# Turning V with VectorE's block transposes instead of TensorE's, in a two-layer trunk

## The chip, the cores and the metric

One Trainium2 core runs the whole program. The metric is the device time of one execution in microseconds, lower is better. The data engines are TensorE (PE; its weight loads are shown apart as PEld), VectorE (DVE), ScalarE (ACT) and GpSimd (POOL). SyncE (SP) issues most loads, GpSimd's queue issues the stores.

## The reference

Input x is 1024 tokens by 1024 features in fp32. Two residual layers follow each other, each with an RMS norm in front:

```python
# layer 0: short gated convolution, width 2048
b, c, u, z = split(h @ w_in, 4)
y = b * conv3(c * u) * silu(z);  x = x + y @ w_out
# layer 1: dilated sliding-window attention, 3 groups (dilation 1, 4, 16) x 16 heads x 64
qkv, z = h @ w_in
q = rms_norm(q) ; k = rms_norm(k)                     # per head
out_g, lse_g = softmax(q k^T / 8 + bias_g) v          # within each group's window and residue classes
o = sum_g softmax_g(lse) * out_g                      # groups merged by their denominators
x = x + (o * silu(z)) @ w_out
```

## The kernel before

Activations lie feature-major: 128 features on the partitions, 1024 tokens along them, worked on in two halves of 512 tokens. The program has four stages: the projections of the convolution layer, its output projection, the projections of the attention layer, and the attention with the last projection.

**Projections.** They are fp32 products made of three reduced-precision ones (high times high, high times low, low times high), and the 2 x 2 blocks of weights and activations are multiplied in Strassen's way with seven products instead of eight. The list `pairs` of the attention layer holds 40 entries. An entry makes two 128-column outputs (`col` 0 and 1) for both halves of the tokens, with seven products of twelve matmuls each (L302, L304, L305). `("qk", hp, g)` gives the query and the key of head pair hp and dilation group g (a unit), `("v", k)` gives the values of two consecutive units, `("z", k)` two gates. The rhythm is qk, qk, v, twelve times, with z entries between. `strassen` runs the products of entry n and makes the weights of entry n + 1 meanwhile: GpSimd forms sums (`sr`, L277), ScalarE the high parts (L165), VectorE the low parts (L166). The products end in VectorE's additions (L314) and ScalarE's copies (L310). The products 4 and 3 of an entry run during the next one.

`between(n, at)` is called after each product and issues the work that is due: `norm` of a qk entry two entries later (per-head norm: a matmul with `swap` into PSUM tile "st", a chain of small VectorE operations, then four times a block transpose of the scales, L712, and the multiplication L724 into the output tile, which GpSimd's queue stores to `qkd`), and four `turn`s of a v entry, also two entries later.

**The values.** Each half of a v output is multiplied by the row scale R1 (1/rms of the token) as it comes out: L684, three of four on GpSimd, one on VectorE, into `spare()`, which is the first half of block tile "blkc"; the norm's output tiles (`out_tile`) are the second half of it. `turn(col, q)` then brings V to token-major: four TensorE transposes of 128 x 128 (L737) into one PSUM bank ("st" for q = 0, "pp" for q = 1), a copy to a tile "f" (ScalarE L742 or VectorE L740), and a store to `vd` (L743). `blk` picks the 128 tokens of a block; for dilation 4 these are every fourth word.

**The row scale.** `stats(1)` computes `rtok` for the second half of the tokens by a chain of VectorE operations on 4 columns (L63 to L67); `spread(1, rtok)` lets TensorE spread it over the partitions into the one bank "st" (L104), which ScalarE copies to R1 (L106). `spread(1, ms2)` does the like for the norm's constant, and `norm` uses the same bank.

**Attention.** `load_v` loads V of a unit, and TensorE loads slices of it as weights, 64 features of one block (L978 for dilations 1 and 4, L971 for 16).

TensorE's order is the order of the code. In the projections the order on the other engines is set by a scheduler that simulates the program, in the attention all orders are written out. The rows of the trace for the groups of 272 matmuls are those of `product`.

Of the kernel before, what the change touches and what calls it, by code (L numbers as in the profile page):

```python
# [19 lines left out]
P = 128  # L20
# [9 lines left out]
G = 3  # L30
# [5 lines left out]
def trunk(ctx: ExitStack, tc: tile.TileContext, a, out):  # L36
# [83 lines left out]
    vd = dram.tile([HP, G, 2, P, HALF], F32, name="vd")  # L120
# [7 lines left out]

    def blk(t, g, b):
        if g == 0:  # L130
            return t[:, b * P:(b + 1) * P]
        if g == 1:
            return t.rearrange("p (n s c) -> p c n s", n=2, c=4)[:, b // 2, b % 2]
        return t[:, b * P:(b + 1) * P]

    with tc.tile_pool(name="wq", bufs=1) as wq, tc.tile_pool(name="sle", bufs=1) as sle, \
# [371 lines left out]
        with tc.tile_pool(name="ev", bufs=1, side="right", reuse_waits="tile") as ev, tc.tile_pool(name="xb", bufs=1, side="right", reuse_waits="tile") as xb, \  # L508
# [150 lines left out]
            def pair(n, w):  # L659
# [4 lines left out]
                def got(col, hf, t, ps=None):  # L664
# [12 lines left out]
                    elif kind == "v":  # L677
                        vt = spare()[:, col * S + hf * HALF:col * S + hf * HALF + HALF]
                        eng, t, r = (nc.vector, ps, R1[:, cs]) if ps is not None else (nc.gpsimd, t, R1[:, cs])
                        if units[p[1] + col][1] == 2:  # L680
                            vt = spare()[:, col * S:col * S + S].rearrange("p (r x i) -> p i x r", r=4, x=4)
                            vt = vt[:, hf * 32:hf * 32 + 32]
                            t, r = (y.rearrange("p (i x r) -> p i x r", x=4, r=4) for y in (t, r))
                        eng.tensor_tensor(vt, t, r, op=OP.mult)  # L684
                    else:
                        if ps is not None:
                            t = ftile()
                            nc.vector.tensor_tensor(t, ps, R1[:, cs], op=OP.mult)
                        else:
                            nc.gpsimd.tensor_tensor(t, t, R1[:, cs], op=OP.mult)  # L690
                        nc.scalar.activation(t, t, AF.Silu)
                        nc.gpsimd.dma_start(zd[p[1] + col, :, cs], t)
# [36 lines left out]
                def turn(col, q):  # L729
                    hp, g = units[p[1] + col]  # L730
                    vt = spare()[:, col * S:col * S + S]
                    if q:
                        pv = cps.tile([P, 4, P], F32, name="pp", tag="pp")
                    else:
                        pv = cst.tile([P, 4, P], F32, name="st", tag="st")
                    for i in range(4):
                        nc.tensor.transpose(pv[:, i], blk(vt, g, 4 * q + i), ident)  # L737
                    o = ftile()
                    if q:
                        nc.vector.tensor_copy(o, pv.rearrange("p a b -> p (a b)"))  # L740
                    else:
                        nc.scalar.activation(o, pv.rearrange("p a b -> p (a b)"), AF.Copy)  # L742
                    nc.gpsimd.dma_start(vd[hp, g, q], o)  # L743
# [39 lines left out]
            def between(n, at):  # L783
# [3 lines left out]
                if n == 1 and at == 0:  # L787
                    stats(1, cst, sm)
                elif n == 2 and at == 2:
                    spread(1, rtok, cst)  # L790
                elif n == 1 and at == 6:
                    spread(1, ms2, cst)
# [30 lines left out]
    with tc.tile_pool(name="sp", bufs=1, space=PSUM) as sp, tc.tile_pool(name="ptp", bufs=2, space=PSUM) as ptp, \  # L823
# [23 lines left out]
        def load_v(hp, g):  # L847
            VS[hp, g] = ap.tile([P, 8, P], F32, name="V", tag="V", bufs=3)
            for q in range(2):
                nc.sync.dma_start(VS[hp, g][:, 4 * q:4 * q + 4].rearrange("p a b -> p (a b)"), vd[hp, g, q])  # L850
# [21 lines left out]
        def attention(hp, g):  # L872
# [24 lines left out]
            def make(js, first):  # L897
# [63 lines left out]
                def C():  # L961
# [4 lines left out]
                    for i, (x, j, vb, f, l) in enumerate(c):  # L966
                        for a in range(2) if g == 2 else ():
                            for s, hs in enumerate((lo, up)):
                                for h in range(2):
                                    rows = slice(64 * h, 64 * h + 64)  # L970
                                    nc.tensor.matmul(u["po", h][hs, (vb + a) * 64:(vb + a) * 64 + 64],  # L971
                                                     V[rows, vb + a, hs], pts[s][rows, i, 64 * a:64 * a + 64],
                                                     start=True, stop=True)
                        for s, hs in enumerate((lo, up)) if g < 2 else ():
# [3 lines left out]
                            nc.tensor.matmul(po[:, j % 4], V[:, vb, hs], pts[s][:, i], start=f, stop=l)  # L978
# [361 lines left out]
```

## Time and profile before

| | |
|---|---|
| median of three runs | 1951.64 us (1950.47 to 1955.07) |
| profiled execution, its span | 1951.91 us, 1950.1 us |
| TensorE, VectorE, ScalarE, GpSimd busy | 98%, 74%, 46%, 43% of the span |
| the turns, in the attention layer's projections | from 902 to 1610 us |
| attention and last projection | from some 1620 us to the end |
| 48 turns on TensorE (L737) | 192 transposes, 29.2 us busy |
| their copies | VectorE 24 x 686 ns, ScalarE 24 x 586 ns |
| stores of V | 48 of 256 KB, 554 ns each on GpSimd |

In a line of the timeline the first number is the start (us from the span's start), the second the duration, and the bracket the idle time before it with what ended it. Rows of the groups give count, busy us and mean ns, and then the idle time in front of them. In the rows by source line the three numbers are the shortest, median and longest duration in ns.

### The profile page before, as it was taken

Reading aid. Unit: us, or ns where it says so; the run is one execution under the profiler, and the core shown is the slowest. Engines: PE = TensorE matmul, PEld = TensorE weight load, DVE = VectorE, ACT = ScalarE, POOL = GpSimd, SP = SyncE. Lnnn points to the kernel's source line nnn. Section 1 sums busy time; section 2 is a strip of 40 time slices with the busy share of each in tenths; the row PEclk is TensorE's granted clock in tenths of the full one; section 3 lists DMA queues with packets and bytes.
Section 4 is the critical chain, followed back from the end, with each engine's and each line's share of the span. In section 5 each row is a group of like instructions: output and inputs, shape, how many; then the busy total and the mean of one; then the engine's idle time right before and its main releaser. Section 6 shows DMA issues by size and latency. Waiting matters only on the chain.

```text
span 1950.1 us, 30571 instructions
## 1 busy us (share of the span) xinstructions
PE 1906.7 (98%) x10894; PEld 1553.0 (80%) x10894; DVE 1443.7 (74%) x2770; ACT 892.3 (46%) x2031; POOL 847.5 (43%) x775
## 2 busy tenths in 40 slices
PE   8999999999999999989999999999999998889999
PEld 6888888888888888878888888888888886667777
DVE  7876766676666655777787588768877776899996
ACT  6433333333333444444444443444344437877780
POOL 0366666666665211424434443444343452333330
PEclk9999999999999999999999999999999999899999
DMA  6312232323223665422332322332232336887852
GB/s 196 121 58 89 88 96 83 99 74 103 76 87 102 222 208 187 140 89 101 106 111 103 114 98 102 115 108 99 92 124 87 130 126 225 251 278 228 245 158 87
DMA packets 117033, 253.79 MB, mean 130 GB/s; under 512 B 17726, under 2 KB 23070, under 8 KB 116880
## 3 DMA queue, kind: packets, MB, share of 16 engines
q1 hardware_dynamic: 93280, 176.89, 28.2%
q0 software_dynamic: 23600, 74.95, 11.3%
q8 instruction: 85, 1.39, 0.3%
q14 instruction: 68, 0.56, 0.1%
HBM read 192.53 MB, written 67.64 MB: 133 GB/s over the span
## 4 chain that ended last, share of the span: by engine, by line
PE 88%; DVE 4%; DMA 4%; ACT 2%; issue 2%; POOL 1%; SPq 0%; DVEq 0%; POOLq 0%; ACTq 0%
PE pp L302 22%; PE pp L304 22%; PE pp L305 22%; PE pp L554 3%; PE pp L555 3%; PE pp L553 3%; ACT xs L950 2%; DMA nld<-nl 2%; PE pp L375 1%; PE pp L376 1%; PE pp L377 1%; PE po L978 1%; PE pt L957 1%; DVE xs L944 1%; DMA ml<-nld 1%
## 5 line engine op out<-in xcount | busy, mean ns | idle before, releaser
L166 DVE TENSOR_TENSOR ws<-wr,ws 128x512 fp32r<-128x512 f32 x284 | 295.4, 1042 | 133.9 <-ACT ws L165 132.0
L165 ACT ACTIVATE ws<-wr 128x512 fp32r<-128x512 f32 x284 | 178.6, 630 | 388.6 <-PE pp L305 254.9
L165 ACT ACTIVATE ws<-sr 128x512 fp32r<-128x512 f32 x272 | 171.6, 631 | 365.9 <-PE pp L305 297.7
L277 POOL TENSOR_TENSOR sr<-wr 128x512 f32<-128x512 f32 x136 | 190.2, 1399 | 266.6 <-DMA wr<-in_wqk 76.5
L166 DVE TENSOR_TENSOR ws<-sr,ws 128x512 fp32r<-128x512 f32 x272 | 219.3, 810 | 84.2 <-ACT ws L165 81.8
L314 DVE TENSOR_TENSOR f<-pp,f 128x512 f32<-128x512 f32 x204 | 140.0, 686 | 105.7 <-PE pp L305 97.8
L950 ACT ACTIVATE xs<-xs,nl 128x256 f32<-128x256 f32 (+2 forms) x384 | 160.5, 424 | 0.0
L310 ACT ACTIVATE f<-pp 128x512 f32<-128x512 f32 x228 | 132.3, 580 | 9.3 <-PE pp L305 9.3
L277 POOL TENSOR_TENSOR sr<-wr,sr 128x512 f32<-128x512 f32 x68 | 88.8, 1306 | 67.9 <-issue 44.1
L944 DVE CUSTOM_DVE_ANT_0 xs<-ps,bt 128x256 f32<-128x256 f32 (+2 forms) x384 | 102.4, 326 | 11.1 <-ACT xs L950 4.4
L302 PE MATMUL pp<-blkf,ws 128*128 128x512 f32 x272 | 108.2, 398 | 0.7 <-ACT f L310 0.7
L302 PE MATMUL pp<-blka,ws 128*128 128x512 f32 x272 | 107.1, 394 | 0.7 <-ACT f L310 0.7
L302 PE MATMUL pp<-blkb,ws 128*128 128x512 f32 x272 | 107.4, 395 | 0.0
L302 PE MATMUL pp<-blkd,ws 128*128 128x512 f32 x272 | 107.3, 395 | 0.0
L305 PE MATMUL pp<-blkf,ws 128*128 128x512 f32 x272 | 106.2, 391 | 0.0
L304 PE MATMUL pp<-blkd,ws 128*128 128x512 f32 x272 | 106.2, 391 | 0.0
L305 PE MATMUL pp<-blkd,ws 128*128 128x512 f32 x272 | 106.1, 390 | 0.0
L304 PE MATMUL pp<-blkf,ws 128*128 128x512 f32 x272 | 106.1, 390 | 0.0
L305 PE MATMUL pp<-blke,ws 128*128 128x512 f32 x272 | 106.1, 390 | 0.0
L305 PE MATMUL pp<-blkb,ws 128*128 128x512 f32 x272 | 106.0, 390 | 0.0
L305 PE MATMUL pp<-blka,ws 128*128 128x512 f32 x272 | 106.0, 390 | 0.0
L302 PE MATMUL pp<-blke,ws 128*128 128x512 f32 x272 | 105.9, 389 | 0.0
(342 smaller groups left out, 5164.1 us busy)
## 6 DMA issues: line engine op xcount, KB each, us to landing
wr<-in_conv_w_in SPq DMA_DIRECT2D x128, 256.0 KB, 3.1
wr<-in_wqk SPq DMA_DIRECT2D x96, 256.0 KB, 3.3
qkd<-blkc POOLq DMA_DIRECT2D x48, 512.0 KB, 3.4
qk<-qkd SPq DMA_DIRECT2D x48, 512.0 KB, 5.4
wr<-in_conv_w_out SPq DMA_DIRECT2D x64, 256.0 KB, 3.2
f<-in_x SPq DMA_DIRECT2D x48, 256.0 KB, 4.4
wr<-in_wv SPq DMA_DIRECT2D x48, 256.0 KB, 3.3
vd<-f POOLq DMA_DIRECT2D x48, 256.0 KB, 2.3
```

The lines of the kernel that those rows point to most:

```text
L165: nc.scalar.activation(t[:, 0], src, AF.Copy)
L166: nc.vector.tensor_tensor(t[:, 1], src, t[:, 0].bitcast(F32), op=OP.subtract)
L277: nc.gpsimd.tensor_tensor(t, x, y, op=op)
L302: nc.tensor.matmul(ps, w[:, 0, ws], b[:, k, 0], start=new and k == 0, stop=False, skip_group_check=not new)
L304: nc.tensor.matmul(ps, w[:, 0, ws], b[:, k, 1], start=False, stop=False, skip_group_check=not new)
L305: nc.tensor.matmul(ps, w[:, 1, ws], b[:, k, 0], start=False, stop=end and k == 3, skip_group_check=not new)
L310: nc.scalar.activation(t, ps, AF.Copy)
L314: nc.vector.tensor_tensor(m, ps, m, op=OP.add)
L553: nc.tensor.matmul(ps[dt], w[:, 0, ws], b[:, k, 0], start=(q == k == 0), stop=False)
L554: nc.tensor.matmul(ps[dt], w[:, 0, ws], b[:, k, 1], start=False, stop=False)
L944: nc.vector.tensor_tensor_reduce(out=x, in0=flat[s][:, cols], in1=u["bt"][s][:, bs], op0=OP.add, op1=OP.min, scale=-1.0, scalar=3e38, accu ...
L950: nc.scalar.activation(x, x, AF.Exp, bias=nm, scale=-1.0, accum_out=L)
```

## The change

- `turn` no longer uses TensorE, PSUM, or ScalarE. One VectorE instruction transposes 32 x 32 blocks of a half of the tile, from `spare()` to `out_tile(col)`. Its outputs lie 8 words apart, so that one tile holds, for each of its partitions, (feature group, feature, block) with the block innermost.
- What the block transpose leaves undone, the 4 x 4 arrangement of the blocks, the store does: after the second half, four stores of 32 partitions each (`a`), in pieces of 256 words (1 KB), in place of two stores of 128 partitions with 2 KB pieces. They are issued by GpSimd, as before.
- The multiplication by R1 (L684) writes the tokens in the order that the transposes want. For dilations 4 and 16 it reads its inputs at steps of 4 and 16 words, and for dilation 16 it becomes two instructions.
- `vd` has one row of 1024 words for each of 128 tokens; V is loaded in two halves of a row, and lies as (feature, block): the weights in the attention are read at a step of 8 words.
- `spread(1, rtok)` comes after product 5 of entry 1, not after product 2 of entry 2: four products sooner in TensorE's order, and ahead of `spread(1, ms2)` and of the first norm.

```diff
-                        vt = spare()[:, col * S + hf * HALF:col * S + hf * HALF + HALF]
+                        vt = spare()[:, col * S:col * S + S]
                         eng, t, r = (nc.vector, ps, R1[:, cs]) if ps is not None else (nc.gpsimd, t, R1[:, cs])
...
+                        if g == 0:
+                            vt = vt.rearrange("p (x n b q) -> p n b x q", x=4, n=2, b=4)[:, hf]
+                            t, r = (y.rearrange("p (b x q) -> p b x q", b=4, x=4) for y in (t, r))
+                        elif g == 1:
+                            vt = vt.rearrange("p (x c n q) -> p n c x q", x=4, c=4, n=2)[:, hf]
+                            t, r = (y.rearrange("p (x q c) -> p c x q", x=4, c=4) for y in (t, r))
+                        if g == 2:
+                            vt = vt.rearrange("p (x n c h q) -> p n h x c q", x=2, n=2, c=4, h=2)[:, hf]
+                            t, r = (y.rearrange("p (q h x c) -> p h x c q", h=2, x=2, c=4) for y in (t, r))
+                            for h in range(2):
+                                eng.tensor_tensor(vt[:, h], t[:, h], r[:, h], op=OP.mult)
...
                 def turn(col, q):
...
-                    for i in range(4):
-                        nc.tensor.transpose(pv[:, i], blk(vt, g, 4 * q + i), ident)
-                    o = ftile()
-                    if q:
-                        nc.vector.tensor_copy(o, pv.rearrange("p a b -> p (a b)"))
-                    else:
-                        nc.scalar.activation(o, pv.rearrange("p a b -> p (a b)"), AF.Copy)
-                    nc.gpsimd.dma_start(vd[hp, g, q], o)
+                    vt = spare()[:, col * S + q * HALF:col * S + q * HALF + HALF]
+                    o = out_tile(col)
+                    nc.vector.transpose(o.rearrange("p (x c b) -> p x b c", x=4, b=8)[:, 2 * q:2 * q + 2],
+                                        vt.rearrange("p (x b q) -> p x b q", x=2, b=8))
+                    if q:
+                        to = vd[hp, g].rearrange("(x q) (a f) -> a q x f", q=32, a=4)
+                        for a in range(4):
+                            nc.gpsimd.dma_start(to[a], o[32 * a:32 * a + 32].rearrange("q (x f) -> q x f", x=4))
...
-                elif n == 2 and at == 2:
+                elif n == 1 and at == 5:
                     spread(1, rtok, cst)
...
-                                                     V[rows, vb + a, hs], pts[s][rows, i, 64 * a:64 * a + 64],
+                                                     V[rows, hs, vb + a], pts[s][rows, i, 64 * a:64 * a + 64],
...
-                            nc.tensor.matmul(po[:, j % 4], V[:, vb, hs], pts[s][:, i], start=f, stop=l)
+                            nc.tensor.matmul(po[:, j % 4], V[:, hs, vb], pts[s][:, i], start=f, stop=l)
```

**TensorE at the second spread.** Before (rows with the numbers of the tiles; L302 to L305 are matmuls of products, "xb" and "blka" to "blkg" the activations):

```order
L304 MATMUL pp_6593<-blka_6512,ws_6559 128x512
L305 MATMUL pp_6593<-blka_6512,ws_6559 128x512
L104 MATMUL st_6852<-ident_67,rtok_79 128x128 x4
L302 MATMUL pp_6768<-xb_5881,ws_6680 128x512
L304 MATMUL pp_6768<-xb_5881,ws_6680 128x512
```

In the changed kernel (line numbers are lower by 7 there):

```order
L297 MATMUL pp_6526<-blkb_6554,ws_6434 128x512
L298 MATMUL pp_6526<-blkb_6554,ws_6434 128x512
L104 MATMUL st_6734<-ident_67,rtok_79 128x128 x4
L295 MATMUL pp_6593<-blkg_6452,ws_6546 128x512
L297 MATMUL pp_6593<-blkg_6452,ws_6546 128x512
```

The spread now stands ahead of the product on "blkg" (the seventh of entry 1); before, it stood ahead of that on "xb" (the sixth of entry 2). Between the two lie the products on "blkg", "blke", "blkf" and "blka".

**VectorE at the first turns.** Before, from the end of the second norm (L724) on:

```order
L724 SCALAR_TENSOR_TENSOR blkc_6798<-f_6749,gain8_74,st_6955 128x128x4
L314 TENSOR_TENSOR f_6877<-pp_6882,f_6877 128x512
L166 TENSOR_TENSOR ws_7061<-sr_7059,ws_7061 128x512
L166 TENSOR_TENSOR ws_7078<-wr_6982,ws_7078 128x512
L314 TENSOR_TENSOR f_7093<-pp_7046,f_7093 128x512
L674 TENSOR_REDUCE st_7002<-f_7096 128x16
L166 TENSOR_TENSOR ws_7101<-sr_7099,ws_7101 128x512
L314 TENSOR_TENSOR f_7117<-pp_7128,f_7117 128x512
L166 TENSOR_TENSOR ws_7125<-wr_7119,ws_7125 128x512
L674 TENSOR_REDUCE st_7142<-f_7143 128x16
L166 TENSOR_TENSOR ws_7154<-wr_7119,ws_7154 128x512
L740 COPY f_7179<-pp_7174 128x512
```

In the changed kernel, from the same place:

```order
L726 SCALAR_TENSOR_TENSOR blkc_6804<-f_6755,gain8_74,st_6955 128x128x4
L307 TENSOR_TENSOR f_6877<-pp_6882,f_6877 128x512
L159 TENSOR_TENSOR ws_7061<-sr_7059,ws_7061 128x512
L735 STREAM_TRANSPOSE blkc_6804<-blkc_6804 128x2x8x32 x2
L159 TENSOR_TENSOR ws_7078<-wr_6982,ws_7078 128x512
L307 TENSOR_TENSOR f_7093<-pp_7046,f_7093 128x512
L735 STREAM_TRANSPOSE blkc_6804<-blkc_6804 128x2x8x32 x2
L159 TENSOR_TENSOR ws_7101<-sr_7099,ws_7101 128x512
```

The first pair of transposes (column 0) stands ahead of the weight split ws_7078 and the addition f_7093, the second (column 1) right behind that addition. The first copy L740 stood eight instructions further back. The first of each two waits for a store (of the norm's result from the same tile) and for GpSimd's or VectorE's L684.

**GpSimd at the first turns.** Before:

```order
L727 DMA qkd_87<-blkc_6798 128x1024
L684 TENSOR_TENSOR blkc_6798<-f_6877,sqacc_81 128x512
L277 TENSOR_TENSOR sr_7182<-wr_7122 128x512
L277 TENSOR_TENSOR sr_7184<-sr_7182,wr_7119 128x512
L277 TENSOR_TENSOR sr_7235<-wr_7119,wr_7122 128x512
L743 DMA vd_88<-f_7151 128x512
```

In the changed kernel:

```order
L729 DMA qkd_87<-blkc_6804 128x1024
L686 TENSOR_TENSOR blkc_6804<-f_6877,sqacc_81 128x4x4x32
L740 DMA vd_88<-blkc_6804 32x4x256 x8
L270 TENSOR_TENSOR sr_7172<-wr_7122 128x512
L270 TENSOR_TENSOR sr_7174<-sr_7172,wr_7119 128x512
```

The stores of V, eight now, stand ahead of the three weight sums of the next entry that they followed before.

More of the change, by code (lines that the diff above doesn't have):

```diff
@@ L119, in trunk @@
     qkd = dram.tile([HP, G, 2, P, S], F32, name="qkd")
-    vd = dram.tile([HP, G, 2, P, HALF], F32, name="vd")
+    vd = dram.tile([HP, G, P, S], F32, name="vd")
     zd = dram.tile([HP, P, S], F32, name="zd")
@@ L677, in got @@
                     elif kind == "v":
-                        vt = spare()[:, col * S + hf * HALF:col * S + hf * HALF + HALF]
+                        vt = spare()[:, col * S:col * S + S]
                         eng, t, r = (nc.vector, ps, R1[:, cs]) if ps is not None else (nc.gpsimd, t, R1[:, cs])
[L680 to L684, printed above, removed]
+                        g = units[p[1] + col][1]
+                        if g == 0:
[9 more added lines that the diff above has]
+                                eng.tensor_tensor(vt[:, h], t[:, h], r[:, h], op=OP.mult)
+                        else:
+                            eng.tensor_tensor(vt, t, r, op=OP.mult)
                     else:
@@ L730, in turn @@
                     hp, g = units[p[1] + col]
-                    vt = spare()[:, col * S:col * S + S]
+                    vt = spare()[:, col * S + q * HALF:col * S + q * HALF + HALF]
+                    o = out_tile(col)
+                    nc.vector.transpose(o.rearrange("p (x c b) -> p x b c", x=4, b=8)[:, 2 * q:2 * q + 2],
+                                        vt.rearrange("p (x b q) -> p x b q", x=2, b=8))
                     if q:
-                        pv = cps.tile([P, 4, P], F32, name="pp", tag="pp")
-                    else:
-                        pv = cst.tile([P, 4, P], F32, name="st", tag="st")
-                    for i in range(4):
-                        nc.tensor.transpose(pv[:, i], blk(vt, g, 4 * q + i), ident)
-                    o = ftile()
-                    if q:
[L740 to L743, printed above, removed]
+                        to = vd[hp, g].rearrange("(x q) (a f) -> a q x f", q=32, a=4)
+                        for a in range(4):
+                            nc.gpsimd.dma_start(to[a], o[32 * a:32 * a + 32].rearrange("q (x f) -> q x f", x=4))
                 if kind == "qk":
@@ L847, in load_v @@
         def load_v(hp, g):
-            VS[hp, g] = ap.tile([P, 8, P], F32, name="V", tag="V", bufs=3)
+            VS[hp, g] = ap.tile([P, P, 8], F32, name="V", tag="V", bufs=3)
             for q in range(2):
-                nc.sync.dma_start(VS[hp, g][:, 4 * q:4 * q + 4].rearrange("p a b -> p (a b)"), vd[hp, g, q])
+                nc.sync.dma_start(VS[hp, g][:, 64 * q:64 * q + 64].rearrange("p a b -> p (a b)"),
+                                  vd[hp, g, :, half(q)])
         banks = [sp.tile([P, 4, P], F32, name="ps", tag=f"ps{i}") for i in range(3)]
```

6 lines of the change are left out of this document (removed).

## The prediction

> **What bounds the kernel now.** I read the page's shares first, then busy time by stage, then TensorE's waits, then the two places that the change touches.
>
> ```profile
> PE 1906.7 (98%) x10894; PEld 1553.0 (80%) x10894; DVE 1443.7 (74%) x2770; ACT 892.3 (46%) x2031; POOL 847.5 (43%) x775
> core 0: us, PE busy (x) PEld busy (x) DVE busy (x) ACT busy (x) POOL busy (x), PEclk, DMA share, GB/s
> 900.00:1600.00 700.00, 700.00 (x3178) 578.34 (x3177) 539.92 (x892) 287.24 (x494) 302.91 (x279) 1.00 0.30 106
> 1630.00:1905.00 275.00, 253.69 (x3378) 193.17 (x3377) 247.81 (x996) 220.61 (x883) 94.52 (x118) 0.97 0.76 228
> ```
>
> From 900 to 1600 us (the projections of the attention layer) TensorE is busy for every microsecond; the list of waits has no wait of TensorE there. So an instruction taken from it there shortens the time by what it occupied, as long as VectorE (540 of 700 us) and GpSimd (303) still keep ahead. From 1630 to 1905 (the attention) TensorE has 254 of 275 us, VectorE 248: neither has much room.
>
> **The turns leave TensorE.** There are 48 turns (12 pairs of V units, two columns, two halves) of four transposes each. Two of them, the first on a unit of dilation 1, the second on one of dilation 4, and the pace of the products around them:
>
> ```profile
> 902.24 0.39 PE L305 MATMUL pp<-blkf,ws 128*128 128x512 f32 x1
> 902.47 0.60 PE L737 MATMUL st<-ident,blkc 128*128 128x128 f32 x4
> 902.82 0.48 PE L302 MATMUL pp<-blka,ws 128*128 128x512 f32 x1
> 903.14 0.39 PE L304 MATMUL pp<-blka,ws 128*128 128x512 f32 x1
> ```
>
> ```profile
> 908.64 0.40 PE L305 MATMUL pp<-xb,ws 128*128 128x512 f32 x1
> 908.88 0.63 PE L737 MATMUL st<-ident,blkc 128*128 128x128 f32 x4
> 909.27 0.48 PE L302 MATMUL pp<-blkd,ws 128*128 128x512 f32 x1
> 909.59 0.40 PE L304 MATMUL pp<-blkd,ws 128*128 128x512 f32 x1
> ```
>
> ```profile
> 846.16 0.39 PE L302 MATMUL pp<-blkg,ws 128*128 128x512 f32 x1
> ...
> 848.65 0.39 PE L305 MATMUL pp<-blkg,ws 128*128 128x512 f32 x1
> ```
>
> Product matmuls start (848.65 - 846.16) / 11 = 0.226 us apart. With four transposes between, two steps take 0.90 us (902.24 to 903.14) where they would take 0.453: a turn costs 0.447 us, and 0.95 - 0.453 = 0.497 for dilation 4. 32 x 0.447 + 16 x 0.497 = **-22.3 us**. This cannot be less than the starts show; if the busy time counted instead (192 x 0.152 = 29 us) it would be more, but those rows overlap their neighbours.
>
> ScalarE's 24 copies out of PSUM (L742) go too; it is 41% busy in this stage (287 of 700), so they count nothing.
>
> **The second spread moves up.** Before, it stands behind the first norm in the use of the one bank "st":
>
> ```profile
> 845.87 0.11 DVE L67 SCALAR_TENSOR_TENSOR rtok<-rtt,rtok 128x4 f32<-128x4 f32 x1
> 857.55 0.39 PE L305 MATMUL pp<-blka,ws 128*128 128x512 f32 x1
> 863.87 0.75 DVE L724 SCALAR_TENSOR_TENSOR blkc<-f,gain,st 128x512 f32<-128x512 f32 x1
> 864.76 1.09 PE L104 MATMUL st<-ident,rtok 128*128 128x128 f32 x4 [6.82 <-DVE blkc L724]
> 865.50 0.78 PE L302 MATMUL pp<-xb,ws 128*128 128x512 f32 x1
> 868.06 0.39 PE L302 MATMUL pp<-xb,ws 128*128 128x512 f32 x1
> 870.37 0.69 DVE L166 TENSOR_TENSOR ws<-sr,ws 128x512 fp32r<-128x512 f32 x1 [5.76 <-ACT ws L165]
> 865.00:867.00 2.00, 2.00 (x8) 1.71 (x8) 0.00 (x0) 0.60 (x1) 0.45 (x1) 0.50 0.91 363
> ```
>
> TensorE stops for 6.8 us until the norm's last multiplication on VectorE gives the bank back, and then runs six matmuls at wide steps (865.50 to 868.06 is 2.56 us where 6 x 0.226 = 1.36 would do; the last row, of the busy times from 865 to 867, has a granted clock of 0.50). Without the wait the matmul of 868.06 would start at 857.55 + 0.226 + 0.45 (the four transposes) + 1.36 = 859.6: **-8.5 us**. In the new place, at what is 846.16 above, the bank is free, the row scale was ready at 845.98 (0.2 us earlier), and ScalarE has a whole product (2.7 us) to empty the bank before the next spread asks for it. Late next: if VectorE is 1 us later with L67, TensorE waits 1 us there. And since VectorE is busy with the norm until 864.6, part of the stall may come back as lateness of its other work: the gain is between 0 and 8.5. I take 8.5, because VectorE then sat idle for 5.76 us up to 870.37, so it has that much to catch up with.
>
> **VectorE's new work.** Nothing in this trace transposes into step-8 outputs. The nearest rows:
>
> ```profile
> L712 DVE STREAM_TRANSPOSE st<-ri 128x512 f32<-128x512 f32 x88 | 63.1, 717 | 1.2
> L724 DVE SCALAR_TENSOR_TENSOR blkc<-f,gain,st 128x512 f32<-128x512 f32 x4 | 4.6, 1144 | 0.1
> L724 DVE SCALAR_TENSOR_TENSOR blkc<-f,gain,st 128x512 f32<-128x512 f32 x4 | 2.9, 735 | 0.1
> L740 DVE COPY f<-pp 128x512 f32<-128x512 f32 x22 | 15.1, 686 | 24.8 <-PE pp L737 24.8
> ```
>
> A transpose of the same size into dense output takes 0.717 us. L724 with dense output (a norm of dilation 1, the second L724 row) takes 0.735, with output in steps of 1 KB (dilation 4, the first) 1.144: 0.41 more for 512 scattered words. So a turn's transpose takes 0.72 to 1.13 us; I take 1.13, for the output is scattered. 48 x 1.13 - 24 x 0.686 (the copies that go) = +37.8 us: 578 of what is then some 678 us, 85%, still with 100 us to spare, 8 for each of the 12 pairs of V. The product with the row scale for dilation 16 splits in two, 4 times on VectorE: under 2 us in all.
>
> More to the point is where the transposes stand and what they wait for. They write the buffer from which the norm's results are being stored (qkd), so they wait for those stores, and for GpSimd's last V product:
>
> ```profile
> 896.36 0.56 POOL L727 DMA_DIRECT2D qkd<-blkc  x1 [0.43 <-DVE blkc L724]
> 896.95 1.39 POOL L684 TENSOR_TENSOR blkc<-f,sqacc 128x512 f32<-128x512 f32 x1
> 898.81 0.68 DVE L314 TENSOR_TENSOR f<-pp,f 128x512 f32<-128x512 f32 x1
> 900.58 0.58 ACT L310 ACTIVATE f<-pp 128x512 f32<-128x512 f32 x1
> 906.00 0.48 PE L302 MATMUL pp<-xb,ws 128*128 128x512 f32 x1
> qkd<-blkc POOLq DMA_DIRECT2D x48, 512.0 KB, 3.4
> ```
>
> In the new order the first two transposes come one weight split ahead of the L314 of 898.81. They can start when L684 ends (898.34), end at 900.6, and with the split between, L314 ends near 902.2 instead of 899.5. The second store lands at 896.36 + 3.4 = 899.8 and holds nobody longer. Behind that L314 queue ScalarE's squares and, behind them, its copy of 900.58, which then ends near 904. The TensorE product that overwrites the copied bank starts at 906.00 (905.1 once two turns are gone): about 1 us of margin. So no stall by the rows, and at most some 2 us for each of 12: 0 to +24, I take **+2**.
>
> **GpSimd.** 96 stores of V where there were 48, plus 12 more products:
>
> ```profile
> L743 POOL DMA_DIRECT2D vd<-f x48 | 26.6, 554 | 58.6 <-DVE f L740 36.2 <-ACT f L742 22.4
> ```
>
> 48 x 0.554 = 27 us, and some 10 for the split products: 303 becomes 340 of 678, no bound. In the new order, though, all eight stores of a pair may come ahead of the weight sums (sr) of the next pair, and wait for the transposes; those sums come up to 5 us later. They are made a whole pair (19 us) before their product, so I put this at nothing; the cover is that lead. The pieces are 1 KB instead of 2 KB, of the same total, with DMA 30% busy.
>
> **What the attention pays.** V now lies with 8 words between neighbouring features, and TensorE loads it as weights, 1376 times:
>
> ```profile
> L978 PEld LDWEIGHTS po<-pts,V x864: 132/137/230, 1630.9 to 1902.0; 128*64 128x64 f32 x173
> L971 PEld LDWEIGHTS po<-pts,V x512: 129/135/228, 1650.2 to 1907.2; 64*64 64x64 f32 x171
> 1748.76 0.85 PEld L978 LDWEIGHTS po<-pts,V 128*64 128x64 f32 x16 [0.28 <-issue]
> 1748.76 1.09 PE L978 MATMUL po<-pts,V 128*64 128x128 f32 x16
> ```
>
> What a step costs shows in the turns, where for dilation 4 the loads read every fourth word (16 bytes). The weight loads of the turns at 902.24 and 908.64:
>
> ```profile
> L737 PEld LDWEIGHTS st<-ident,blkc 128*128 128x128 f32 x4 | 0.5, 139 | 0.1
> L737 PEld LDWEIGHTS st<-ident,blkc 128*128 128x128 f32 x4 | 0.6, 204 | 0.1
> ```
>
> 65 ns more for 128 columns, 33 for V's 64. All of it exposed: 1376 x 33 = 45 us. But of the 65 only 12 reached the matmuls (0.05 us for four, above), the rest went beside the matmul in front: 1376 x 6 = 8 us. Below that end: sixteen V loads follow each other every (0.85 - 0.137) / 15 = 48 ns, so these ordinary loads take at least 0.74 ns a column, where the strided ones of the turns took (204 - 139) / 128 = 0.5 more than theirs; if an ordinary load is slow enough already to hide a new step, 0. So 0 to 45, I take **+8**, from the only row with a step.
>
> On this the Trainium skill speaks against the change: SBUF — State Buffer, in its section "Door 1: The DMA port swizzle", says that SBUF is read in lines of 16 bytes, and that each access that crosses to a new line pays, so that four fp32 is as far as one strides for free. By that each of V's columns starts a new line and pays in full, the 45 us of the rival below; the dilation 4 turns, at just 16 bytes, already paid (204 against 139 ns), so the trace agrees that the step costs load time, but not that it reaches the matmuls.
>
> **The sum**, on the profiled execution (1951.9 us, 1950.1 of it span; the median of the runs is 1951.6): 1951.9 - 22.3 - 8.5 + 2 + 8 = 1931.1; I say **1931**.
>
> **Rivals.**
> 1. *Strided weights (the other side).* Each V load delays its matmul by the full 33 ns: 1951.9 - 30.8 + 2 + 45 = 1968. For it: TensorE is at 92% in that stage, so little hides. Against: the 12 of 65. It decides from 29 / 1376 = 21 ns a load upward. By half (16 ns) it ends near 1945.
> 2. *VectorE becomes the late engine.* The wait for stores and GpSimd, then 2.3 us of transposes at a stretch, twice a pair, use up the 1 us margin, and TensorE stops for some 2 us in each of 12 pairs: +24, 1931 + 22 = 1953, no change. For it: VectorE goes to 85%, in bursts. Against: TensorE waits nowhere in 900 to 1600 today, with VectorE idle for 160 us of it.
> 3. *The spread brings nothing:* the bank's wait only moves to the next user of "st" (ms2's spread or the norm). 1931 + 8.5 = 1940.
>
> **Chances.** Forecast with rival 3 inside it (1920 to 1943) 0.66; something of rivals 1 and 2 (1943 to 1948) 0.14; rival 2 in full or a half-exposed load plus stalls (1948 to 1956) 0.07; rival 1 in full 0.13. Faster means by over 0.2%, 3.9 us, about what a measurement of this kernel can tell: 0.80; same 0.07; slower 0.13. The low end is everything gained and nothing paid, 1921, less a little for the pace of the turns: 1919. The high end leaves rival 1 and half of rival 2 out: 1951.
>
> **What the profile after would show.** No L737-like transposes on TensorE, and 0.226 us steps throughout the projections; no wait of several us before the spread; VectorE's transposes near 1.1 us (0.72 would say that a step is free); TensorE still without waits up to the end of the projections, which then end some 30 us earlier; V's weight loads at 137 to 170 ns, and the stretch from there to the end longer by 0 to 16 us. Wrong I would be if V's groups of sixteen take well over 1.02 us, or if TensorE waits for ScalarE's copies near each turn.

## The result, and the profile after

| | before | changed |
|---|---|---|
| median of five runs each | 1952.13 us (1950.47 to 1955.19) | 1936.95 us (1932.72 to 1942.0) |
| ratio, 95% interval | | 0.9912 (0.9893 to 0.9932) |
| profiled execution, its span | 1951.91, 1950.1 us | 1936.95, 1935.2 us |

It became faster by 15 us (by the ratio, whose estimate is not that of the two medians, by 17), where 21 were forecast. Shares and busy time by stage of the changed kernel (columns as in the prediction: PE, PEld, DVE, ACT, POOL busy, granted clock, DMA share, GB/s):

```profile
PE 1894.8 (98%) x10702; PEld 1550.5 (80%) x10702; DVE 1474.2 (76%) x2798; ACT 878.5 (45%) x2007; POOL 902.4 (47%) x835
860.00:900.00 40.00, 40.00 (x178) 32.94 (x177) 35.67 (x57) 15.67 (x28) 18.93 (x21) 1.00 0.37 128
900.00:1590.00 690.00, 689.22 (x3041) 566.89 (x3041) 583.38 (x918) 275.16 (x472) 357.84 (x342) 1.00 0.34 112
1596.00:1604.00 8.00, 2.76 (x30) 1.62 (x30) 2.76 (x16) 4.47 (x15) 0.00 (x0) 0.51 0.66 226
1615.00:1890.00 275.00, 256.43 (x3293) 204.63 (x3291) 237.25 (x972) 213.94 (x853) 93.64 (x117) 0.98 0.74 221
```

The projections look as forecast: TensorE full, VectorE at 85% of the stage, no stall in 860 to 900. What no line of the prediction had is the fourth row: right behind the projections TensorE works 2.76 of 8 us, at a clock of 0.51.

To see where the 15 us come from, two marks common to all kernels are enough: the first spread of `rtok` (first start in the row of L104) and the last product matmul of the projections. The first mark by source line (after the three durations stand the first and the last start), before:

```profile
L104 PE MATMUL st<-ident,rtok x8: 271/347/445, 770.3 to 865.4; 128*128 128x128 f32 x8
```

and in the changed kernel:

```profile
L104 PE MATMUL st<-ident,rtok x8: 271/272/294, 771.2 to 847.4; 128*128 128x128 f32 x8
```

The second from the timeline, before:

```profile
1620.93 0.39 PE L305 MATMUL pp<-blkb,ws 128*128 128x512 f32 x1
```

Mark to mark: 850.6 before, 820.2 after, **-30.4 us** (the forecast's two gains make -30.8). From the last product to the end of the span: 329.2 before, 343.9 after, **+14.7 us**. The changed kernel reaches the first mark 0.9 us later. The gain arrived whole; half of it was given back in the attention. TensorE's two largest waits there (in all, times, longest):

```profile
PE ps L929 <- DVE nl L942: 13.2, 3, 7.5
PE pt L955 <- DVE pts L866: 10.8, 7, 4.2
```

The timeline of the changed kernel shows the second mark and, behind it, the longest of these waits:

```profile
1591.35 0.39 PE L298 MATMUL pp<-blkb,ws 128*128 128x512 f32 x1
...
1592.09 0.86 PE L929 MATMUL ps<-qk 64*64 64x192 f32 x10
1594.77 0.57 POOL L694 DMA_DIRECT2D zd<-f  x1 [0.96 <-ACT f L693]
1599.72 0.29 DVE L942 CUSTOM_DVE_ANT_0 xs<-ps,bt 128x128 f32<-128x128 f32 x1 [7.25 <-DMA zd<-f]
1600.41 1.60 PE L929 MATMUL ps<-qk 64*64 64x192 f32 x16 [7.46 <-DVE nl L942]
...
1608.59 1.00 PE L976 MATMUL po<-pts,V 128*64 128x128 f32 x12
```

The first score is computed at 1592.09. VectorE's instruction that negates it into the first tile "xs", and writes the largest value of each row, negated, into the small tile "nl" (L942), then waits 7.25 us until the last gate store, `zd`, issued at 1594.77, has landed; TensorE's next scores wait for that instruction. Before, the same instruction ran at once, 2.1 us ahead of the last `zd` store:

```profile
1622.28 0.29 DVE L944 CUSTOM_DVE_ANT_0 xs<-ps,bt 128x128 f32<-128x128 f32 x1 [0.23 <-PE ps L931]
1624.35 0.57 POOL L692 DMA_DIRECT2D zd<-f  x1 [0.96 <-ACT f L691]
```

The two have nothing to do with each other but memory: z tiles come from the twelve buffers of "f", and tiles of the attention lie over some of these. In the two programs' lists of instructions (before, then after) the semaphores that this instruction waits on, and the queue lane of the last `zd` store, show it:

```
L944 ISA xs,nl<-ps,bt 128x128 [waits DMASW5,DMASW1,DMAHW6,DVE,PE]
L942 ISA xs,nl<-ps,bt 128x128 [waits DMASW2,DVE,DMAHW6,PE,Activation]
L694 DMA zd<-f 128x512 [waits DMASW2,Activation]     (the last one)
```

The addresses of the tiles in the two programs tell which tile it is. The first "xs" lies over "blka" in both. The first "nl", 128 bytes of each partition from 224992 on, lies inside the tenth of the twelve "f" buffers (2048 bytes from 223168 on) in both. Before, two of the turns' V tiles had that buffer last, and their stores (lanes 1 and 5) stand ahead of the last four gate stores in GpSimd's order. With the turns gone from "f", the tile of the last `zd` store has it (lane 2). A lane alone does not name a store; the address does.

The other part is V. Loads of V as weights in the changed kernel, by source line (shortest, median, longest ns), and then the two groups of matmuls with V by form (count, busy us, mean ns):

```profile
L976 PEld LDWEIGHTS po<-pts,V x864: 194/212/226, 1608.6 to 1886.0; 128*64 128x64 f32 x173
L969 PEld LDWEIGHTS po<-pts,V x512: 191/213/227, 1629.0 to 1892.1; 64*64 64x64 f32 x171
```

```profile
L976 PE MATMUL po<-pts,V 128*64 128x128 f32 x864 | 70.8, 303 | 2.5 <-DVE o L988 2.4
L969 PE MATMUL po<-pts,V 64*64 64x64 f32 x512 | 19.7, 279 | 0.4 <-DVE o L991 0.4
```

The same groups before:

```profile
L978 PE MATMUL po<-pts,V 128*64 128x128 f32 x864 | 63.3, 286 | 4.0 <-DVE o L990 4.0
L971 PE MATMUL po<-pts,V 64*64 64x64 f32 x512 | 13.0, 226 | 1.8 <-DVE o L993 1.8
```

A load went from 137 and 135 to 212 and 213 ns. TensorE's busy time with V grew by 70.8 + 19.7 - 63.3 - 13.0 = 14.2 us, 10 ns for each of 1376 loads.

### The profile page after: what moved, and what is told of

Same layout as the page of the kernel before. It is cut to its first block, busy times and chain, and to the rows that moved or that the text cites. A ratio compares the mean times of both kernels' runs of the same rounds, so it can differ in the third digit from the quotient of the medians.

```text
span 1935.2 us, 30212 instructions
## 1 busy us (share of the span) xinstructions
PE 1894.8 (98%) x10702; PEld 1550.5 (80%) x10702; DVE 1474.2 (76%) x2798; ACT 878.5 (45%) x2007; POOL 902.4 (47%) x835
## 4 chain that ended last, share of the span: by engine, by line
PE 89%; DVE 3%; DMA 3%; issue 2%; ACT 1%; POOL 1%; SPq 0%; DVEq 0%; POOLq 0%; ACTq 0%
PE pp L295 22%; PE pp L297 21%; PE pp L298 21%; PE pp L547 3%; PE pp L548 3%; PE pp L546 3%; PE po L976 2%; PE pt L955 2%; DMA nld<-nl 2%; PE pp L368 1%; PE pp L369 1%; PE pp L370 1%; PE ps L929 1%; PE pd L1150 1%; PE pd L1152 1%
## 5 line engine op out<-in xcount | busy, mean ns | idle before, releaser
L159 DVE TENSOR_TENSOR ws<-sr,ws 128x512 fp32r<-128x512 f32 x272 | 225.9, 836 | 84.6 <-ACT ws L158 82.6
L270 POOL TENSOR_TENSOR sr<-wr 128x512 f32<-128x512 f32 x136 | 195.0, 1434 | 198.5 <-DMA wr<-in_conv_w_in 68.0
L942 DVE CUSTOM_DVE_ANT_0 xs<-ps,bt 128x256 f32<-128x256 f32 (+2 forms) x384 | 102.8, 325 | 19.3 <-DMA zd<-f 7.2
L295 PE MATMUL pp<-blka,ws 128*128 128x512 f32 x272 | 105.9, 389 | 0.7 <-ACT f L303 0.7
L295 PE MATMUL pp<-blkg,ws 128*128 128x512 f32 x272 | 105.9, 389 | 0.0
```

The costliest lines, as they stand in the source:

```text
L159: nc.vector.tensor_tensor(t[:, 1], src, t[:, 0].bitcast(F32), op=OP.subtract)
L270: nc.gpsimd.tensor_tensor(t, x, y, op=op)
L295: nc.tensor.matmul(ps, w[:, 0, ws], b[:, k, 0], start=new and k == 0, stop=False, skip_group_check=not new)
L942: nc.vector.tensor_tensor_reduce(out=x, in0=flat[s][:, cols], in1=u["bt"][s][:, bs], op0=OP.add, op1=OP.min, scale=-1.0, scalar=3e38, accu ...
```

## The experiments

The theory: the turns and the spread each gave what they promised; the first score's wait for the last `zd` store took some 8 us of it back; V at step 8 took 4 to 6. The rivals: the spread brought nothing by itself; the start's wait is for a load; V's price is 0, or the whole 75 ns a load. Ratios are to the kernel before on the same chip. "Between marks" and "to the end" are the two stretches above, read in each run's profile in the same way.

| kernel | median us | ratio, interval | between marks | to the end |
|---|---|---|---|---|
| before | 1952.13 | | 850.6 | 329.2 |
| changed | 1936.95 | 0.9912, 0.9893 to 0.9932 | 820.2 | 343.9 |
| 1 spread alone | 1946.52 | 0.9964, 0.9951 to 0.9978 | 842.2 | 329.7 |
| 2 turns alone | 1947.55 | 0.9960, 0.9946 to 0.9974 | 830.1 | 343.4 |
| 3 one more f tile | 1927.75 | 0.9865, 0.9850 to 0.9880 | 820.0 | 334.3 |
| 4 V read densely | 1933.15 | 0.9891, 0.9874 to 0.9907 | 820.1 | 342.3 |
| 5 both of 3 and 4 | 1925.10 | 0.9855, 0.9842 to 0.9867 | 819.8 | 330.3 |
| 6 before, V at step 8 | 1959.09 | 1.0029, 1.0019 to 1.0040 | 850.8 | 336.9 |
| 7 transposes twice | 1939.68 | 0.9927, 0.9915 to 0.9939 | 825.5 | 339.6 |
| 8 eight more f tiles | 1935.63 | 0.9911, 0.9898 to 0.9924 | 820.1 | 343.9 |
| 9 V at step 4 | 1931.35 (one run) | | 820.0 | 337.8 |
| 10 V at step 2 | 1929.18 (one run) | | 819.9 | 337.4 |
| 11 two blocks innermost | 1932.70 | 0.9898, 0.9879 to 0.9917 | 819.5 | 340.3 |
| 12 one more f tile, again | 1929.01 | 0.9876, 0.9863 to 0.9890 | 820.0 | 336.9 |

The stretch between the marks repeats within 0.4 us among kernels that share its code (the changed one, 3 to 5 and 8 to 10, 12). The stretch to the end does not: the same kernel (3 and 12) gave 334.3 and 336.9.

**1 and 2: the two parts apart.** In 1, on the kernel before:

```diff
-                elif n == 2 and at == 2:
+                elif n == 1 and at == 5:
                     spread(1, rtok, cst)
```

> The kernel before with only the second spread of rtok five products sooner; the 48 turns stay on TensorE and V is read as before. Theory (the spread's stall and the slow clock behind it were worth 8.5 us by themselves): about 1943.5 us against 1952, ratio 0.9956; TensorE busy 40 of 40 us in 860 to 900 at a clock of 1.00, last projection matmul about 8 us earlier than 1620.9. Rival (the bank's wait only moves to the next user of st, as long as turns use st too): 1952, the wait of about 7 us is found on another line.

In 2 the same lines go back in the changed kernel.

> The changed kernel with the second spread of rtok put back at its old place; turns on VectorE and step-8 V stay. Theory (the two parts add): about 8.5 us over the changed kernel, 1945.5, and the projections end about 8 us later than 1591.4, with a wait of the spread's transposes on VectorE's sum of 5 to 7 us. Rival (with the turns gone from st the spread's stall is gone too, so moving it brings nothing): 1937, no wait in 860 to 900.

The spread alone takes 850.6 - 842.2 = 8.4 us out of the stretch between the marks, the turns 842.2 - 820.2 = 22.0 (from 1 to the changed kernel). With the turns alone the stall is there, a little longer than before. The spread's place in 2:

```profile
867.27 1.08 PE L104 MATMUL st<-ident,rtok 128*128 128x128 f32 x4 [7.79 <-DVE blkc L726]
```

In the changed kernel it starts without a wait:

```profile
847.05 0.62 PE L104 MATMUL st<-ident,rtok 128*128 128x128 f32 x4
```

In the other order the turns give 850.6 - 830.1 = 20.5 and the spread 830.1 - 820.2 = 9.9, so the split is known to some 1.5 us. In 1 the whole time fell by 7 us. (By TensorE's order, shown above, the spread moved by four products; the "five" of the expectation is a slip.) So both rivals on the spread fall, and the parts add within the intervals: 0.9964 x 0.9960 = 0.992, against 0.9912. Kernel 1 has before's stretch to the end, 2 the changed kernel's: the loss in the attention belongs to the turns.

**3 and 8: the start of the attention.** In 3, in `between` of the attention layer's projections; 8 has `range(8)`:

```diff
+                if n == len(pairs) - 1 and at == 2:
+                    for _ in range(1):
+                        nc.gpsimd.memset(ftile()[:, :1], 0.0)
```

> The changed kernel with one more tile taken from the ring of f buffers near the end of the projections (a memset of one column on GpSimd and nothing else), so that the memory of the first tile of negated scores is no longer that of the last stored z tile. Theory (the 7.25 us wait of the first score's VectorE instruction is for that store to land): the wait goes, TensorE's wait at the first score falls from 7.5 us to under 1.5, and the time falls by 6 to 8 us, to about 1930. Rival (it waits for a slow load of the bias, of q and k, or for ScalarE's table): the wait stays with another releaser, and the time stays at 1937.

> Like the kernel with one more f tile, but with eight, so that the ring of twelve turns on until the first tile of negated scores lies again on a buffer that a late z store reads. Theory (it is the memory that couples them): the wait of some 7 us at the first score is back, and the time is 1937, as in the changed kernel. Rival (the additional memset or the changed order of GpSimd took the wait away): no wait, 1928.

VectorE's first score instruction in 3:

```profile
1592.90 0.29 DVE L945 CUSTOM_DVE_ANT_0 xs<-ps,bt 128x128 f32<-128x128 f32 x1 [0.33 <-PE ps L932]
```

In 8:

```profile
1599.98 0.29 DVE L945 CUSTOM_DVE_ANT_0 xs<-ps,bt 128x128 f32<-128x128 f32 x1 [8.83 <-DMA zd<-f]
```

One more tile and the wait is gone, with 9.2 us of the median (7.9 in the repeat, 12). Eight more and it is back, with the time of the changed kernel. The same extra kind of instruction stands in both, so it is the memory. The addresses agree: in 3 the extra tile itself takes the buffer under "nl" and the last z tile another one; in 8 that z tile has it again. The tile concerned is "nl", beside the tile of negated scores that the expectation names. How much it cost can be read at the first matmul with V, which in 3 is this one:

```profile
1601.39 1.00 PE L979 MATMUL po<-pts,V 128*64 128x128 f32 x12
```

It starts 9.9 us behind the last product (1591.45), in the changed kernel 17.2 (1608.59 - 1591.35): 7.3 us. In the profiles of the seven kernels with this wait (changed, 2, 4 and 7 to 10) it is 17.2 to 19.5 us, in the seven without it 9.9 in each: the wait costs 7.3 to 9.6 us there. Kernel 3 is the fastest of those that compute the whole result.

**4, 5 and 6: the price of V.** In 4 (and in 5, on kernel 3), and in 6 on the kernel before, which gets `"p (c b) -> p b c", b=8`:

```diff
-                    V = VS[hp, g]
+                    V = VS[hp, g].rearrange("p a b -> p (a b)").rearrange("p (v c) -> p c v", v=8)
```

> The changed kernel with the V weights read contiguously from the tile as it lies (so that it multiplies the wrong V values: this one leaves the right order of V out), everything else the same. Theory (64-column loads at a step of 32 bytes take 212 in place of 137 ns, of which 9 to 11 ns come out per load, 1376 loads): loads fall back to about 137 ns, groups of sixteen from 1.17 to 1.02 us, time 8 to 15 us less than the changed kernel, about 1925. Rival A (all of the 75 ns is exposed): 100 us less. Rival B (loads are hidden behind matmuls everywhere, and the longer stretch after the projections has only the wait at its start as cause): 1937, no change.

> Both of the last two edits in the changed kernel: one more f tile near the end of the projections, and V weights read contiguously (wrong V values: the right order of V is left out). The two traces so far: dense V took 14 us of TensorE's busy time away (63.3 + 13.3 in place of 70.8 + 19.7 us in the two groups of matmuls with V), but 7 us of new waits for VectorE came in their place. Theory (two thirds of the V price is covered, since VectorE is next in line in this stage): 3 to 6 us under the kernel with the buffer edit alone, 1922 to 1925 on its scale of 1927.75. Rival (the cover came only from the late start, and with the start mended all 14 us come out): 1914.

> The kernel before with nothing changed but the V weights read at a step of 32 bytes from the tile as it lies (wrong V values: the right order of V is left out). Theory (the price of the step is 4 to 6 us of time, 14 us of TensorE's busy time): 1956 to 1958 on before's scale of 1952, loads at 212 ns, the two groups of matmuls with V 14 us longer in sum. Rival (fully exposed busy time): 1966. Rival (nothing): 1952.

The groups of V in 4, by form:

```profile
L976 PE MATMUL po<-pts,V 128*64 128x128 f32 x864 | 63.3, 286 | 3.7 <-DVE o L988 3.6
L969 PE MATMUL po<-pts,V 64*64 64x64 f32 x512 | 13.3, 232 | 1.4 <-DVE o L991 1.4
```

and in 6:

```profile
L978 PE MATMUL po<-pts,V 128*64 128x128 f32 x864 | 70.4, 302 | 2.7 <-DVE o L990 2.7
L971 PE MATMUL po<-pts,V 64*64 64x64 f32 x512 | 20.2, 283 | 1.3 <-DVE o L993 1.2
```

The 14 us of busy time in V's groups go with the dense read and come with the strided one, whatever else is changed. The time follows by less: 1.0029 x 1952 = +5.7 us in 6 (+3.7 to +7.8), and, from the ratios, 0.9912 to 0.9891 = -4 us in 4, 0.9865 to 0.9855 = -2 us in 5, each within the intervals of the pair it compares, so that only 6 shows the price by itself. Two things lie between. The groups' rows overlap with others of TensorE: from the last product to the end its busy time as a whole (the first number behind the length) grew by 11 us, before and in 6:

```profile
1620.93:1950.10 329.17, 301.84 (x3730) 231.38 (x3728) 284.28 (x1076) 228.72 (x905) 96.36 (x120) 0.97 0.69 211
1621.60:1958.50 336.90, 312.94 (x3730) 248.45 (x3728) 285.50 (x1076) 228.82 (x905) 96.38 (x120) 0.97 0.67 206
```

And TensorE idled less, 24.0 in place of 27.3 us. The other way round, where it is done sooner, it waits for VectorE. The largest such wait in 3, then in 5:

```profile
PE pt L958 <- DVE pts L869: 7.8, 6, 4.4
PE pt L958 <- DVE pts L869: 12.2, 9, 4.5
```

In 4 it is 13.4 us, in the changed kernel 10.8. The expectation of 8 to 15 us for 4 was too high for these reasons. By 6 both extremes fall: it is neither nothing nor the whole.

**9 and 10: which step costs.** As 4, but with pieces of 4 and 2 words:

```diff
-                    V = VS[hp, g]
+                    V = VS[hp, g].rearrange("p a b -> p (a b)").rearrange("p (v c b) -> p v c b", v=2, b=4)
...
-                            nc.tensor.matmul(po[:, j % 4], V[:, hs, vb], pts[s][:, i], start=f, stop=l)
+                            nc.tensor.matmul(po[:, j % 4], V[:, vb // 4, hs, vb % 4], pts[s][:, i], start=f, stop=l)
```

> The changed kernel with V weights read at a step of 16 bytes (4 elements) in place of 32 (wrong V values: the right order of V is left out). What is asked is the time of one load. Theory A (the price comes as a jump once neighbouring elements no longer share a line of 16 bytes, so that at 16 and at 32 bytes each element is a line of its own): 212 ns, as at 32 bytes. Theory B (it grows with the bytes that are passed over): about 169 ns, which is 137 + 75 x 3/7.

> The changed kernel with V weights read at a step of 8 bytes (2 elements; wrong V values: the right order of V is left out). Theory A (each element's share of a 16-byte line counts, two elements to a line): half the way, about 174 ns, or 137 ns if only the 64 bytes and more of a row count. Theory B (it grows with the bytes that are passed over): about 148 ns, which is 137 + 75/7.

Loads at 16 bytes (9):

```profile
L976 PEld LDWEIGHTS po<-pts,V x864: 192/209/231, 1609.0 to 1880.4; 128*64 128x64 f32 x173
```

Loads at 8 bytes (10):

```profile
L976 PEld LDWEIGHTS po<-pts,V x864: 135/138/231, 1608.1 to 1879.2; 128*64 128x64 f32 x173
```

137, 138, 209, 212 ns at 4, 8, 16 and 32 bytes: a jump between 8 and 16, as theory A has it with 137 for two words to a line. The Trainium skill (SBUF — State Buffer, section "Door 1: The DMA port swizzle") says that a 16-byte line needs two hits or more for full bandwidth, which fits these four numbers; its next sentence, that four fp32 may be strided for free, is one step too far here. The times of 9 and 10, of one run each, say nothing of V's price: 9, whose loads pay in full, ran faster than any run of the changed kernel.

**7: VectorE's reserve.**

```diff
-                    nc.vector.transpose(o.rearrange("p (x c b) -> p x b c", x=4, b=8)[:, 2 * q:2 * q + 2],
-                                        vt.rearrange("p (x b q) -> p x b q", x=2, b=8))
+                    for _ in range(2):
+                        nc.vector.transpose(o.rearrange("p (x c b) -> p x b c", x=4, b=8)[:, 2 * q:2 * q + 2],
+                                            vt.rearrange("p (x b q) -> p x b q", x=2, b=8))
```

> The changed kernel with each of the 48 block transposes of VectorE done twice (+48 x 1.16 = +56 us of VectorE's work during the projections). Theory (VectorE has 107 us to spare of 690 there, and TensorE waits for it nowhere): no change, 1937 within 3 us, no new wait of TensorE between 900 and 1590. Rival (VectorE's reserve is used up by bursts, so that more work comes out at products that wait for an eviction): up to 56 us more, waits of pp for DVE at L295.

The median came 2.7 us above the changed kernel's, within what was expected, but the stretch between the marks is 5.3 us longer, and against the expectation there are new waits. Waits of TensorE in 7:

```profile
PE pp L295 <- ACT f L303: 4.3, 5, 1.0
...
PE st L698 <- DVE st L667: 1.4, 2, 1.2
```

Of 56 us more work on VectorE a tenth comes out. The first row is TensorE waiting for ScalarE's copies, which stand behind VectorE's work, the place that the prediction's second rival named; with one transpose that wait is 1.4 us (2 times), as before the change. The second row, a wait for VectorE itself in the norm, is new. Why the stretch to the end is 4.3 us shorter in 7 stays open. Behind the first matmul with V, the profiles of the seven kernels with V at step 8 (changed, 2, 3, 6, 7, 8, 12) are 1.3 to 7.8 us longer than before's, 7 being the shortest: a single profile does not size V.

**11 and 12: two blocks innermost.** On kernel 3, V's rows as (block pair, feature, block of the pair), so that both the transposes' outputs and the weights have a step of 8 bytes; the pieces of the stores are 256 bytes, and V is loaded in four parts of 32 partitions.

```diff
-                    nc.vector.transpose(o.rearrange("p (x c b) -> p x b c", x=4, b=8)[:, 2 * q:2 * q + 2],
-                                        vt.rearrange("p (x b q) -> p x b q", x=2, b=8))
+                    nc.vector.transpose(o.rearrange("p (y c b) -> p y b c", y=16, b=2)[:, 8 * q:8 * q + 8],
+                                        vt.rearrange("p (y b q) -> p y b q", y=8, b=2))
...
-            for q in range(2):
-                nc.sync.dma_start(VS[hp, g][:, 64 * q:64 * q + 64].rearrange("p a b -> p (a b)"),
-                                  vd[hp, g, :, half(q)])
+            for x in range(4):
+                nc.sync.dma_start(VS[hp, g][32 * x:32 * x + 32].rearrange("r y a b -> r (y a b)"),
+                                  vd[hp, g].rearrange("(r x) s -> x r s", x=4)[x])
```

> The kernel with one more f tile (1927.75 us), and V laid out with two blocks innermost in place of eight: transposes with outputs at a step of 8 bytes, stores in pieces of 256 bytes (16 for each partition in place of 4 of 1 KB), loads of V as four of 32 partitions, weights at a step of 8 bytes. Nothing of the result is left out. Theory (loads at a step of 8 bytes cost nothing, 138 ns; the price of step 8 was 2 to 6 us; the transfers are hidden, DMA being a third busy in the projections): V's two groups of matmuls 14 us shorter, time 1922 to 1926. Rival (pieces of 256 bytes take so long to land that the last V stores, or GpSimd's issues, come out at TensorE): 1930 or more, with a new wait that has vd or V in its name. The transposes: about 1.16 us as before if any step costs, about 0.72 if, as for the weights, 8 bytes is free.

> The kernel with one more f tile again, beside the last one on the same chip: 1927.75 us within 3 us by every theory; its difference from the one with two blocks innermost is what is asked.

The theory failed: 1932.7 against 1929.0 us on the same chip. The expected gain is not there; the two intervals just overlap, so that a loss is not sure. What the theory said of the transposes and of V's groups held. The transposes by source line, the groups of V by form, and a row of the waits of the queue that issues the loads, in 11:

```profile
L735 DVE STREAM_TRANSPOSE blkc<-blkc x48: 659/677/716, 892.1 to 1572.5; 128x512 f32<-128x512 f32 x48
```

```profile
L979 PE MATMUL po<-pts,V 128*64 128x128 f32 x864 | 63.6, 287 | 2.6 <-DVE o L991 2.5
L972 PE MATMUL po<-pts,V 64*64 64x64 f32 x512 | 14.1, 243 | 1.8 <-DVE o L994 1.8
```

```profile
SPq L886 <- DMA qk<-qkd: 23.0, 12, 5.5
```

The transposes fell from 1.16 to 0.68 us and V's groups by 12.3 us of busy time (from 70.4 + 19.6 in 12). What took the gain away is in the stretch to the end, 340.3 against 336.9 in 12. The queue waited 23.0 us for earlier loads of q and k; in 12 it was 7.8:

```profile
SPq L886 <- DMA qk<-qkd: 7.8, 3, 4.4
```

No wait on vd or V stands in TensorE's list, so the rival's sign is not there either. That twice as many loads hold up that queue, and so the bias loads behind (L886), fits these rows, but it may not be the queue alone: the DMA engines were busy for 0.75 of that stretch against 0.67 in 12, at nearly the same GB/s (204 and 206), and VectorE waited 17.0 us (4 times) against 5.8 (3 times) for small loads of `ml` (L1018) that GpSimd's queue issues. None of it was tried by itself; the cause stays open.

## Why the prediction was right, and where not

It said 1931 and faster; the measured 1937 lies 6 us above, inside the range. The gain came by the mechanism that it gave. That the total stayed inside is in part luck: the range was kept wide for rivals that came at most in part, and it covered a wait that had no term. By its steps:

- **The turns, -22.3.** Measured 22.0 (20.5 by 2). The pace of the matmul starts was the right measure, not the 29 us of busy time.
- **The second spread, -8.5.** Measured 8.4 by 1 (9.9 by 2). VectorE being busy with the norm gave nothing of it back. Rival 3 did not come.
- **VectorE's lateness, +2.** It is already in the turns' 22.0, so 0.3 by that order of the parts, and at most 1.8 by the other. The transposes took what was estimated, 1.16 us against 1.13. Their line in the changed kernel:

```profile
L735 DVE STREAM_TRANSPOSE blkc<-blkc x48: 1129/1156/1260, 891.3 to 1573.8; 128x512 f32<-128x512 f32 x48
...
its engine sat idle before it (us, times) until:
  POOL blkc L686: 4.7, 4
who waited for it (us, times):
  POOL vd L740: 40.2, 16
```

VectorE idled 4.7 us ahead of them, for GpSimd's product; behind them wait GpSimd's stores, 40 us, and TensorE for none of it. Rival 2's mechanism is real, but needs twice this load to cost 5 us (7).
- **GpSimd, 0.** Right in effect; 358 of 690 us busy against an estimate of 340 of 678. That products read at a step cost more was not counted. The first pair of V in the timeline of the changed kernel, a unit of dilation 1 and one of dilation 4 (inputs at 16 bytes):

```profile
859.68 1.29 POOL L686 TENSOR_TENSOR blkc<-f,sqacc 128x512 f32<-128x512 f32 x1
872.42 2.14 POOL L686 TENSOR_TENSOR blkc<-f,sqacc 128x512 f32<-128x512 f32 x1 [3.76 <-DVE f L307]
```

The Trainium skill (GPSIMD Engine Reference, section "7. Performance pitfalls for Q7 kernels") has half as much again for reads at a step of more than 8 bytes; the trace agrees in the sign and has two thirds more.
- **V's weights, +8.** The sum was near (2 to 8 us by 4, 5 and 6), its working was not. The load grew by 75 ns, not by 33: the step that failed is "65 ns more for 128 columns, 33 for V's 64". A turn's load belongs to a transpose, V's to a matmul, and the quoted rows had a transpose's 128 columns at 139 ns, as long as V's 64 at 137: halving had no ground. Loads of one kind do go by columns, as those of q in the attention before show (64 columns, then 128, all without a step):

```profile
L931 PEld LDWEIGHTS ps<-qk x704: 129/133/228, 1621.7 to 1887.2; 64*64 64x64 f32 x176
L926 PEld LDWEIGHTS ps<-qk x160: 182/186/335, 1621.2 to 1879.2; 64*128 64x128 f32 x160
```

The prediction's own sign of being wrong came: a group of sixteen V matmuls takes 1.24 us in a row of the timeline, 1.09 before. V's groups paid 10 ns a load, not 6, 14.2 us in sum. Of that TensorE's whole busy time shows 11 us in 6, and its waits were some 3 us shorter there, a cover that the prediction did not count. Rival 1 would have needed 33 ns exposed.
- **What had no term: the first score's wait, +7.3** (at the first matmul with V in the profiled run, up to 9.6 in others; 9.6 and 7.0 by the last column of the table, against 3 and 12). The prediction counted the ring "f" only as instructions that go, and looked for new waits only behind the instructions that were added. It was to be had beforehand from the list of instructions, where the first score's instruction waits on the lane of the last `zd` store, and from the addresses. Its "0 to 16 us longer to the end" held the 14.7 by luck, since that was meant for V alone.

With it the sum is -22.0 - 8.4 + 7.3 + 2 to 8 for V, from -21 to -15, against -15.2 by the medians and -17 by the ratio (-13 to -21). In the profiled run 14.7 - 7.3 = 7.4 us lie behind that matmul, so V is put at the upper end there; the profile of 3 has 5.1 in the whole stretch, that of 12 has 7.7, so part of it is scatter.

The change takes 48 tiles, four times twelve, out of "f", so a strict ring of twelve buffers would have ended at the same place. By the addresses it is not one: in the changed program the last sixteen tiles of "f" have the tenth buffer three times and the eleventh not at all. How a buffer is picked stays open.

## What to carry to other kernels

Where a change takes tiles out of a shared pool, read in the new list of instructions what the first users of that memory in the next stage wait for: one dummy tile was worth 7 to 9 us, half the whole gain. A cost has to be followed through: here 75 ns on a load's own row were 10 ns at the matmuls and some 4 in the time, because TensorE's rows overlap and VectorE stood next in line. And a duration measured on one kind of instruction is carried over to another, by size or otherwise, only if rows of both kinds show that it goes that way.

## What the runs showed of the hardware

- Weight loads of fp32 at steps of 4, 8, 16 and 32 bytes took 137, 138, 209 and 212 ns, for a matmul's 64 columns on 128 partitions; a transpose's 128 columns took 139 ns without a step and 204 at 16 bytes. Loads of q without a step, on 64 partitions, took 133 ns for 64 columns and 186 for 128.
- VectorE's 32 x 32 transposes of 128 x 512 fp32 took 0.68 us into outputs at a step of 8 bytes and 1.16 us at 32 bytes; 0.72 into PSUM without a step.
- A GpSimd product of 128 x 512 took 1.29 us with dense inputs and 2.14 with inputs at 16 bytes; one of 128 x 256 at 64 bytes had a median of 1.31:

```profile
L684 POOL TENSOR_TENSOR blkc<-f,sqacc x24: 1196/1310/1696, 918.3 to 1551.5; 128x256 f32<-128x256 f32 x24
```

- Behind the wait at the first score TensorE's granted clock was 0.50 for 4 us and 0.70 for 4 more:

```profile
1600.00:1604.00 4.00, 2.76 (x30) 1.62 (x30) 2.47 (x16) 3.99 (x15) 0.00 (x0) 0.50 0.35 132
1604.00:1608.00 4.00, 4.00 (x38) 2.79 (x32) 2.82 (x14) 2.74 (x12) 0.00 (x0) 0.70 0.00 0
1608.00:1612.00 4.00, 4.00 (x48) 3.47 (x50) 3.32 (x19) 4.00 (x17) 0.90 (x1) 1.00 0.64 176
```
